# Linear layers whose products are traced one group behind the split of their weights

## The chip, the cores and the metric

The program runs on one core of a Trainium2 chip. The metric is the device time of one execution in microseconds (us), the median of three runs. Engines are named as the profile names them: PE (TensorE, matmuls), PEld (its weight loads), DVE (VectorE), ACT (ScalarE), POOL (GpSimd), SP (SyncE, whose queue issues most DMAs).

## The reference, cut to what matters

256 tokens of width 1024 go through a hybrid layer (an SSD scan and a sparse attention side by side, then a mixture of 32 experts of which each token takes 2) and through two layers of a second block for the tokens and for a context of 256 (grouped attention, then latent attention, each with a gated convolutional feed-forward part of width 2816). What matters here is that nearly all of it is matrix products with float32 weights from DRAM, and that the experts' products are small:

```python
for e in range(N_EXPERTS):
    he = jax.nn.silu(t @ w_g[e]) * (t @ w_u[e])
    out = out + combine[:, e:e + 1] * (he @ w_d[e])
```

The kernel computes an expert only for the tokens that chose it, 32, 64 or 128 positions for each.

## The kernel before, in words

**A linear layer.** Weights come in groups. `weight` (L183) loads a tile of 128 x 512 float32 (256 KB) through SP's queue into a ring of 14 buffers named `raw`. `split_weight` (L188) turns a group into a high part (`whi`, L198, on ACT) and the rest (`wlo`, L199, on DVE); both rings have 4 buffers (L106), and a group of a linear layer takes two of each. `mm3` (L214) then makes three products for each block: `whi` x high activations (L217), `wlo` x high (L218), `whi` x low (L219). `lin_fm` (L221) puts features on partitions: chunks of 256 columns, groups of 4 blocks of 128 rows, so 24 products a group and two groups for an inner size of 1024. `lin_tm` (L247) puts tokens on partitions, in groups of 1024 // width blocks. The products add up in the PSUM ring `lin`.

**Evictions.** A finished chunk isn't evicted at once. Its eviction is put on the list `late`, and `flush` (L204), at the end of the next `split_weight` or at the end of the layer, traces it. So the order of tracing is: split of a group, eviction of the chunk that ended before it, products of the group.

**Side work.** Each linear layer is a generator that yields the PE time it has traced. `weave` (L137) and `mix` (L157) put units of other generators between its steps in fixed shares: the scan, the sparse attention, the columns of the adaptive norms (`ada_quad`, L385), the attentions. In one stretch the roles are turned: `mix(self.experts(), (ctx, 2.1))` (L1930) makes the experts the main work and the context's linear layers (`layer0_ctx`, L1663, with `residual` and `ffn`) the side work. A unit of four experts of 32 positions (`expert_block`, L1306, products at L1317 and L1339) is two rounds of four products, one in each of the four column tiles of PE (128 x 32 weights). Their weights (`wx`, L1302) come through SP's queue too. In this part of the program the ring `lin` has two PSUM banks (L1922), later four (L1935).

**What sets the order.** Tracing gives each instruction its rank. A list scheduler then lays out each engine's stream ahead of time: an instruction that it takes to be ready may pass one of an earlier rank that it takes to be waiting. Each engine executes its stream in that order.

The functions that the change touches, with the line numbers of the profile:

Of the kernel before, what the change touches and what calls it, by code (L numbers as in the profile page):

```python
# [16 lines left out]
P = 128  # L17
# [71 lines left out]
# The experts by their rank in number of tokens: the order of the units (rank of group, half) and their blocks.  # L89
# [3 lines left out]
# The 8 KB buffers: those of the second part lie where what the first part keeps there is done early.  # L93
# [5 lines left out]
class Kernel:  # L99
    def __init__(self, tc, I, cst, cst_at, out, dbg=None):  # L100
        self.tc, self.nc, self.I, self.out = tc, tc.nc, I, out
        self.cst_ap, self.cst_at = cst, cst_at
        self.dbg = dbg or (lambda name, ap: None)
        self.V, self.A, self.T, self.G, self.S = (
            tc.nc.vector, tc.nc.scalar, tc.nc.tensor, tc.nc.gpsimd, tc.nc.sync)
        self.bufs = {"raw": 14, "whi": 4, "wlo": 4, "k2": 8, "k1": 5, "s": 11}  # L106
        self.marks, self.late = [], []
        self.room, self.turn = 0, 0
        self.phase_pool, self.phase_bufs = None, {}
# [60 lines left out]
    def passing(self, name, tag):  # L170
        """A constant that is needed only once."""
# [10 lines left out]
    # ---------------------------------------------------------------- weights  # L182
# [5 lines left out]
    def split_weight(self, view):  # L188
        """(hi, lo) of each block of 128 rows of a view [128, n, cols]."""
# [11 lines left out]
        self.flush()  # L201
        return parts

    def flush(self):  # L204
        """Evictions are traced after the next weights' split, which TensorE waits for."""
# [15 lines left out]
    def lin_fm(self, W, c0, ncols, act, evict, k0=0, nk=None, more=False):  # L221
        """out^T: features on partitions. W [K, N] in DRAM; act (hi, lo) [128, nk, 256]."""
        hi_a, lo_a = act
        nk = nk or W.shape[0] // P
        for cc in range(0, ncols, 256):
            ps = self.ps("lin", [P, 2, TOK])
            for kg in range(0, nk, 4):
# [4 lines left out]
                for k in range(n):  # L232
                    for m in range(2):
                        ms = slice(m * P, m * P + P)
                        self.mm3(ps[:, m, :], (parts[k][0][:, ms], parts[k][1][:, ms]), (hi_a[:, kg + k, :], lo_a[:, kg + k, :]),
                                 kg + k == 0 and m == 0, kg + k == nk - 1)
                if kg + n < nk:
                    yield n * 0.66
            def out(cc=cc, ps=ps):
                for m in range(2):  # L240
                    evict(cc // P + m, ps[:, m, :])
            self.late.append(out)
            if cc + 256 >= ncols and not more:
                self.flush()
            yield n * 0.66

    def lin_tm(self, W, c0, ncols, act, evict, chunk=512):  # L247
        """out: tokens on partitions."""
        hi_a, lo_a = act
        nk = W.shape[0] // P  # L250
        for cc in range(0, ncols, chunk):
            w = min(chunk, ncols - cc)
            pss = [self.ps("lin", [P, w]) for _ in range(2)]
            step = 1024 // w
            for kg in range(0, nk, step):
# [3 lines left out]
                for k in range(n):  # L259
                    for t in range(2):  # L260
                        s = slice(t * P, t * P + P)
                        self.mm3(pss[t], (hi_a[:, kg + k, s], lo_a[:, kg + k, s]), parts[k],
                                 kg + k == 0, kg + k == nk - 1)
                if kg + n < nk:
                    yield n * w * 0.0025
            def out(cc=cc, w=w, pss=pss):
                for t in range(2):
                    evict(t, cc, w, pss[t])
            self.late.append(out)
            if cc + w >= ncols:  # L270
                self.flush()
            yield n * w * 0.0025

    # ---------------------------------------------------------------- set-up
# [73 lines left out]
    def load_fm(self, src, h, tag, eng):  # L348
        """[256, 1024] rows of DRAM -> feature-major h [128, 8, 256]."""
# [16 lines left out]
    # ---------------------------------------------------------------- adaLN  # L366
# [11 lines left out]
    def take_bias(self, stg, dst):  # L378
        """The bias into dst [128, slots, 48], to which the products are added."""
# [5 lines left out]
    def ada_quad(self, W, q, dst, rsel):  # L385
        """Columns 2048q..2048q+2047 of silu(c) @ W onto dst [128, slots, 48]."""
# [17 lines left out]
    def ada_start(self, p):  # L404
        """Shift and scale of the first norm for half of the features, in the order of ada1."""
# [20 lines left out]
    def first_act(self, rb):  # L426
        """The first norm and the first two chunks of the token-major projection, by halves of the features as the
        modulation comes in."""
# [4 lines left out]
        def products(half):  # L433
            for c in range(2):
                for k0 in range(4 * half, 4 * half + 4, 2):
                    parts = self.split_weight(W[k0 * P:k0 * P + 2 * P, 5120 + 468 * c:5588 + 468 * c].rearrange(
                        "(k p) n -> p k n", p=P))
                    for k in range(2):
                        for t in range(2):
                            ts = slice(t * P, t * P + P)  # L440
                            self.mm3(pss[c][t], (act[0][:, k0 + k, ts], act[1][:, k0 + k, ts]), parts[k],
                                     k0 + k == 0, k0 + k == 7)
                        yield 1.2
# [32 lines left out]
    # ---------------------------------------------------------------- norms  # L476
    def square_sums(self, h, nt, st, gain=None):
        """Sums of squares over features (32 times them) into the two columns of st: the column tiles of TensorE add up
        a quarter each."""
# [17 lines left out]
    def rms_bcast(self, h, nt, dim):  # L497
        """1/rms over features, one column per token, on all partitions (PSUM [128, 256])."""
# [11 lines left out]
    def spread(self, r, n):  # L510
        """Columns of r, one value per token, along the free dimension of all partitions."""
# [11 lines left out]
    def modulation(self, gain, ada, slot, vs, vsc):  # L523
        """gain * (1 + scale) and shift, [128, 8] each."""
# [15 lines left out]
    # ---------------------------------------------------------------- first block: projections  # L540
# [26 lines left out]
    def rope(self, x, nh, t, outs):  # L567
        """x [128, nh, 64] token-major, half-split rotation; written to each of outs."""
# [12 lines left out]
    def project_tm(self, act, pss):  # L581
        """dt, q, k/v, gates of the first block, tokens on partitions; the first two chunks are in pss."""
# [8 lines left out]
    def conv_silu(self, dst, ps, wname, bname, m, nm, taps):  # L591
        """Causal depthwise convolution over tokens, then silu."""
# [20 lines left out]
    # ---------------------------------------------------------------- SSD  # L613
# [40 lines left out]
    def ssd(self):  # L654
        """The chunked scan; y (with the skip) replaces the x channels. Yields where TensorE would wait."""
# [90 lines left out]
    def ssd_gate(self, act, sums):  # L746
        """y * silu(z), and its squares summed by group into sums [2][128, 2, 256]."""
# [35 lines left out]
    # ---------------------------------------------------------------- NSA  # L783
# [141 lines left out]
    def nsa_attend(self):  # L925
        """Selected and window branches (causal both: every block is chosen and the window spans the sequence)."""
# [85 lines left out]
    def tanh_gates(self, act, c0, sg):  # L1012
        """tanh(x / 2): the sigmoid is half of one more."""
# [78 lines left out]
    # ---------------------------------------------------------------- mixture of experts  # L1092
    def router(self, h):
# [35 lines left out]
        def top(x):  # L1129
            """softmax over the 8 columns; its sorted values and their places."""  # L1130
# [55 lines left out]
        # experts by their number of tokens: place of each expert and expert of each place  # L1186
# [67 lines left out]
    def one_hots(self, d, cols):  # L1254
        """For positions 256 d + cols: token x position, by first and second choice, [128, 2, n] per half of tokens."""
# [10 lines left out]
    def expert_gather(self, d, tag, n=256):  # L1266
        """The normalised tokens at positions 256 d.., features on partitions."""
# [15 lines left out]
    def expert_weights(self, part, experts):  # L1283
        """One part of the experts' weights, 256 rows of gate or up or 256 columns of down each."""
# [21 lines left out]
    def expert_block(self, xg, d, q, experts, sizes):  # L1306
        """The 128 positions 256 d + 128 q..: one expert's, or several experts' in the column tiles of TensorE."""
# [42 lines left out]
    def expert_spread(self, d, q):  # L1350
        """What takes the block's rows back to the tokens, position x token, and the rows' weights."""
# [29 lines left out]
    def experts(self):  # L1381
        """The two experts with the most tokens have 128 positions each, the next two 64, the others 32."""
# [13 lines left out]
    def experts_rest(self):  # L1396
        """Tokens beyond those positions: blocks of 32 from position 1536."""
# [580 lines left out]
```

## Time and profile before

| | us |
|---|---|
| runs, median of 3 (lowest, highest) | 1768.83 (1765.71, 1769.4) |
| profiled execution, first to last instruction | 1765.9 |
| PE busy | 1690.6 (96%) |
| DVE, ACT busy | 1272.3 (72%), 917.8 (52%) |

The profile has no other time of the profiled execution than its span; the median of the runs lies 2.9 us above it. PE's busy time is the union of its matmuls, which are pipelined: a product of 256 columns is shown with 0.28 us, and the next begins 0.12 us after it began. A matmul of the experts, whose operands are plain float32, stands in the trace as two records; in the order below it is one row.

### The profile page before, as it was taken

To read this page: it belongs to the slowest core of one execution; us is meant where nothing else is said; L and a number is where in the kernel's file an instruction comes from. 1 tells how busy PE (TensorE), PEld (TensorE's weight loads), DVE (VectorE), ACT (ScalarE), POOL (GpSimd) and SP (SyncE) were. 2 spreads that over 40 slices of the span, in tenths; PEclk is the share of its full clock that TensorE was granted. 3 is DMA by queue.
4 is the path that set the end of the run, shared out by engine and by line. 5 is a ranking of instruction groups with operands and counts; after the bars stand their busy time and mean duration, and the time that the engine had idled before them with its cause. 6 is when DMAs were issued, how large, how long until landed. Compare 5 with 4: busy or idle time off the path is not lost. (4 is left out here: it accounts for less than half of the span.)

```text
span 1765.9 us, 36466 instructions
## 1 busy us (share of the span) xinstructions
PE 1690.6 (96%) x12980; PEld 1379.4 (78%) x12980; DVE 1272.3 (72%) x3070; ACT 917.8 (52%) x1901; POOL 42.4 (2%) x48
## 2 busy tenths in 40 slices
PE   7999999999999999999999898999999989999998
PEld 3898777767876578888887554688999866789997
DVE  3997687675667768757756466968777788777876
ACT  2666446863443544534434252656665566556654
POOL 0000000100001000000000001000000000000000
PEclk8999999999999999999999988999999999999999
DMA  9756956849966997998999886234566432246662
GB/s 321 212 150 195 322 175 191 253 133 306 317 201 207 323 318 240 329 328 268 325 347 346 258 299 229 90 122 138 178 183 183 141 120 72 59 141 183 180 186 72
DMA packets 344962, 381.54 MB, mean 216 GB/s; under 512 B 27353, under 2 KB 298454, under 8 KB 344774
## 3 DMA queue, kind: packets, MB, share of 16 engines
q1 hardware_dynamic: 339456, 376.47, 67.2%
q10 hardware_dynamic: 5174, 1.97, 0.4%
q8 instruction: 104, 1.70, 0.4%
q0 software_dynamic: 144, 0.71, 0.1%
q14 instruction: 84, 0.69, 0.1%
HBM read 378.00 MB, written 1.05 MB: 215 GB/s over the span
## 5 line engine op out<-in xcount | busy, mean ns | idle before, releaser
L198 ACT CAST whi<-raw 128x512 fp32r<-128x512 f32 (+2 forms) x752 | 453.9, 610 | 383.9 <-PE lin L219 219.5
L199 DVE TENSOR_TENSOR wlo<-raw,whi 128x512 fp32r<-128x512 f32 (+2 forms) x752 | 502.4, 678 | 161.5 <-ACT whi L198 148.6
L217 PE MATMUL lin<-XA,whi 128*128 128x256 f32 x768 | 220.1, 287 | 1.7 <-ACT XA L465 1.7
L219 PE MATMUL lin<-XA,whi 128*128 128x256 f32 x768 | 219.0, 286 | 0.0
L218 PE MATMUL lin<-XA,wlo 128*128 128x256 f32 x768 | 218.9, 285 | 0.0
L217 PE MATMUL lin<-A,whi 128*128 128x256 f32 x576 | 168.4, 292 | 2.7 <-DVE k L598 1.9
L218 PE MATMUL lin<-A,wlo 128*128 128x256 f32 x576 | 163.5, 284 | 0.0
L217 PEld LDWEIGHTS lin<-XA,whi 128*128 128x128 f32 x768 | 149.3, 194 | 2.6 <-ACT XA L465 2.5
L218 PEld LDWEIGHTS lin<-XA,wlo 128*128 128x128 f32 x768 | 149.2, 194 | 0.7 <-issue 0.4
L219 PEld LDWEIGHTS lin<-XA,whi 128*128 128x128 f32 x768 | 148.9, 194 | 0.3
L217 PEld LDWEIGHTS lin<-A,whi 128*128 128x128 f32 x576 | 109.9, 191 | 33.8 <-issue 14.1
L219 PE MATMUL lin<-A,whi 128*128 128x256 f32 x448 | 127.7, 285 | 0.0
L217 PE MATMUL lin<-CA,whi 128*128 128x256 f32 x416 | 122.0, 293 | 0.3 <-ACT whi L198 0.2
L218 PE MATMUL lin<-CA,wlo 128*128 128x256 f32 x416 | 118.2, 284 | 1.1 <-DVE wlo L199 1.1
L219 PE MATMUL lin<-CA,whi 128*128 128x256 f32 x416 | 117.9, 283 | 0.0
L218 PEld LDWEIGHTS lin<-A,wlo 128*128 128x128 f32 x576 | 110.1, 191 | 0.9 <-issue 0.7
L1621 ACT ACTIVATE cv<-lin,vecs 128x256 f32<-128x256 f32 x132 | 73.9, 560 | 63.0 <-PE lin L219 52.7
L219 PE MATMUL lin<-XB,whi 128*128 128x256 f32 x352 | 99.4, 286 | 0.1
L1622 DVE SCALAR_TENSOR_TENSOR cv<-lin,vecs,cv 128x255 f32<-128x255 f32 x132 | 63.3, 480 | 49.4 <-ACT cv L1621 49.1
L217 PE MATMUL lin<-XB,whi 128*128 128x256 f32 x352 | 98.7, 283 | 0.0
L218 PE MATMUL lin<-XB,wlo 128*128 128x256 f32 x352 | 98.4, 283 | 0.0
L217 PEld LDWEIGHTS lin<-CA,whi 128*128 128x128 f32 x416 | 79.2, 190 | 15.5 <-issue 6.5
(534 smaller groups left out, 3835.0 us busy)
## 6 DMA issues: line engine op xcount, KB each, us to landing
raw<-in_ffn_w_up_dram SPq DMA_DIRECT2D x264, 256.0 KB
raw<-in_ada_w_dram SPq DMA_DIRECT2D x192, 256.0 KB
raw<-in_ffn_w_down_dram SPq DMA_DIRECT2D x132, 256.0 KB
raw<-in_w_in_dram SPq DMA_DIRECT2D x112, 256.0 KB
wx<-in_w_exp_gate_dram SPq DMA_DIRECT2D x112, 256.0 KB
wx<-in_w_exp_up_dram SPq DMA_DIRECT2D x112, 256.0 KB
wx<-in_w_exp_down_dram SPq DMA_DIRECT2D x112, 256.0 KB
raw<-in_w_ada_dram SPq DMA_DIRECT2D x96, 256.0 KB
```

The lines of the kernel that those rows point to most:

```text
L198: self.A.copy(hi, raw)
L199: self.V.tensor_tensor(lo, raw, hi.bitcast(F32), OP.subtract)
L217: mm(out, whi, ahi, start=first, stop=False, skip_group_check=True)
L218: mm(out, wlo, ahi, start=False, stop=False, skip_group_check=True)
L219: mm(out, whi, alo, start=False, stop=last, skip_group_check=True)
L1621: A.activation(acc, ps, AF.Identity, bias=self.v(f"fb{i}", m), scale=self.v(f"fw{i}1", m))
L1622: V.scalar_tensor_tensor(acc[:, 1:], ps[:, 0:TOK - 1], self.v(f"fw{i}0", m), acc[:, 1:], OP.mult, OP.add)
```

## The change

Each group is split first; then what an earlier group has left to evict is traced; then the products of the group before. So products are traced one group later than the split of their weights, and the eviction of a finished chunk is traced after the split of the group after the next. `behind` keeps the last group's products in `self.ahead`; `settle`, at the end of a layer that isn't followed by more of it, traces what is left. The list is one for all generators, so the split of one layer can bring out the products of another. `lin_tm` takes at most two blocks in a group, which differs for 288 columns alone (three blocks before). The diff, cut to its core (it takes out comments and docstrings too):

```diff
@@ split_weight
             parts += [(hi[:, j, :], lo[:, j, :]) for j in range(m)]
+        return parts
+
+    def behind(self, products):
         self.flush()
-        return parts
+        last, self.ahead = self.ahead, products
+        if last:
+            last()
+
+    def settle(self):
+        self.behind(None)
+        self.flush()
@@ lin_fm
+        def products(cc, kg, n, parts, held):
+            if kg == 0:
+                held.append(self.ps("lin", [P, 2, TOK]))
+            ps = held[0]
+            for k in range(n):
+                for m in range(2):
...
+            if kg + n == nk:
+                self.late.append(lambda: [evict(cc // P + m, ps[:, m, :]) for m in range(2)])
         for cc in range(0, ncols, 256):
-            ps = self.ps("lin", [P, 2, TOK])
+            held = []
             for kg in range(0, nk, 4):
                 n = min(4, nk - kg)
                 r0 = (k0 + kg) * P
                 parts = self.split_weight(
                     W[r0:r0 + n * P, c0 + cc:c0 + cc + 256].rearrange("(k p) n -> p k n", p=P))
...
-            if cc + 256 >= ncols and not more:
-                self.flush()
-            yield n * 0.66
+                self.behind(lambda a=(cc, kg, n, parts, held): products(*a))
+                if kg + n == nk and cc + 256 >= ncols and not more:
+                    self.settle()
+                yield n * 0.66
@@ lin_tm (otherwise as lin_fm)
-            step = 1024 // w
+            step = min(2, 1024 // w)
@@ first_act, products(half)
-                    for k in range(2):
...
-                        yield 1.2
+                    self.behind(some)
+                    yield 2.4
+            self.settle()
@@ experts_rest
+        self.settle()
         total = self.nc.values_load(self.over[0:1, 16:17], min_val=0, max_val=16)
```

Every engine executes the same instructions before and after but for ACT, which loads its function table two times less. The order differs. On PE, near the end of the experts' stretch, a unit of gate or up products of four experts (`acc<-wx,xg`) stood in one piece between the context's products (`lin<-CA`) before:

```order
L218 MATMUL lin<-CA_8571,wlo 128x256
L219 MATMUL lin<-CA_8572,whi 128x256
L1317 MATMUL acc<-wx,xg 32x256 x8
L217 MATMUL lin<-CA_8571,whi 128x256
L218 MATMUL lin<-CA_8571,wlo 128x256
L219 MATMUL lin<-CA_8572,whi 128x256
```

In the changed kernel single products of such a unit stand between the context's products (`lin<-CB`, the same layers a little later) there:

```order
L1332 MATMUL acc<-wx,xg 32x256
L227 MATMUL lin<-CB_11924,whi 128x256
L1332 MATMUL acc<-wx,xg 32x256
L228 MATMUL lin<-CB_11924,wlo 128x256
L229 MATMUL lin<-CB_11925,whi 128x256
L227 MATMUL lin<-CB_11924,whi 128x256
L228 MATMUL lin<-CB_11924,wlo 128x256
L229 MATMUL lin<-CB_11925,whi 128x256
L227 MATMUL lin<-CB_11924,whi 128x256
L228 MATMUL lin<-CB_11924,wlo 128x256
L1332 MATMUL acc<-wx,xg 32x256
L229 MATMUL lin<-CB_11925,whi 128x256
```

From the last unit that stands alike in both to the end of the context's work, the same 128 expert products stood in 18 runs before and stand in 44 runs now. Counted in rounds (up to four products that follow each other, one for each column tile), they are 36 before and 61 now. In the whole program the runs of these products (with weights `wx`) go from 100 to 128, the rounds from 288 to 313. The order of the loads in SP's queue is the same in that stretch.

On DVE, where the latent attention's projection of the context (288 columns) begins beside the first feed-forward part, the low parts of the first weights stood like this before, after the last pieces of the norm (`CA`) and between evictions (`hx`):

```order
L466 SCALAR_TENSOR_TENSOR CA_15970<-k_15995,ada_69,CA_15969 128x256
L1089 SCALAR_TENSOR_TENSOR hx<-lin,ada_68,hx 128x256
L466 SCALAR_TENSOR_TENSOR CA_15970<-k_15999,ada_69,CA_15969 128x256
L1089 SCALAR_TENSOR_TENSOR hx<-lin,ada_68,hx 128x256
L199 TENSOR_TENSOR wlo<-raw,whi 128x288 x2
```

They are the second and the third tile of a group of three. Now a group has two, both stand ahead of the evictions:

```order
L481 SCALAR_TENSOR_TENSOR CA_15945<-k_15970,ada_69,CA_15944 128x256
L199 TENSOR_TENSOR wlo<-raw,whi 128x288
L481 SCALAR_TENSOR_TENSOR CA_15945<-k_15974,ada_69,CA_15944 128x256
L199 TENSOR_TENSOR wlo<-raw,whi 128x288
L1104 SCALAR_TENSOR_TENSOR hx<-lin,ada_68,hx 128x256 x2
```

The splits have moved ahead of two evictions of the other layer. On PE nothing but a handful of neighbours changes places in the two feed-forward parts of the tokens (about 1230 to 1406 us and from 1540 us to the end in the profile before).

## Rows read from the trace of the kernel before

**Rows 1.** The page, part 1: busy time, share and instructions of each engine.

```profile
PE 1690.6 (96%) x12980; PEld 1379.4 (78%) x12980; DVE 1272.3 (72%) x3070; ACT 917.8 (52%) x1901; POOL 42.4 (2%) x48
```

**Rows 2.** Stretches of the program: busy us of each engine, clock, DMA share.

```profile
core 0: us, PE busy (x) PEld busy (x) DVE busy (x) ACT busy (x) POOL busy (x), PEclk, DMA share, GB/s
0.00:44.00 44.00, 32.38 (x206) 16.28 (x207) 14.46 (x43) 11.89 (x21) 1.64 (x6) 0.88 0.91 321
...
860.00:933.00 73.00, 73.00 (x714) 62.24 (x713) 47.34 (x102) 29.22 (x54) 0.00 (x0) 1.00 1.08 339
933.00:997.00 64.00, 60.81 (x575) 47.93 (x577) 38.10 (x84) 22.94 (x45) 0.00 (x0) 1.00 1.06 340
997.00:1012.00 15.00, 10.95 (x110) 5.50 (x102) 6.75 (x16) 1.76 (x3) 0.00 (x0) 0.97 0.59 185
...
1230.00:1406.00 176.00, 175.96 (x1441) 174.28 (x1440) 137.62 (x269) 108.45 (x206) 0.00 (x0) 1.00 0.58 174
```

**Rows 3.** Waits of PE in the whole span: us in total, times, longest.

```profile
PE lin L219 <- DVE wlo L199: 4.4, 4, 2.7
...
PE lin L218 <- DVE wlo L199: 1.1, 2, 0.9
...
PE lin L217 <- ACT whi L198: 0.9, 2, 0.7
```

**Rows 4.** Timeline of PE around a whole expert unit: start, us, line.

```profile
886.44 0.28 PE L218 MATMUL lin<-CB,wlo 128*128 128x256 f32 x1
886.56 0.28 PE L219 MATMUL lin<-CB,whi 128*128 128x256 f32 x1
886.77 1.07 PE L1317 MATMUL acc<-wx,xg 128*32 128x256 f32 x16
887.77 0.39 PE L217 MATMUL lin<-CB,whi 128*128 128x256 f32 x1
888.00 0.28 PE L218 MATMUL lin<-CB,wlo 128*128 128x256 f32 x1
```

**Rows 5.** Timeline of PE around one round of an expert unit.

```profile
974.31 0.28 PE L219 MATMUL lin<-CB,whi 128*128 128x256 f32 x1
974.52 0.64 PE L1317 MATMUL acc<-wx,xg 128*32 128x256 f32 x8
975.09 0.38 PE L217 MATMUL lin<-CB,whi 128*128 128x256 f32 x1
975.31 0.28 PE L218 MATMUL lin<-CB,wlo 128*128 128x256 f32 x1
975.52 0.63 PE L1317 MATMUL acc<-wx,xg 128*32 128x256 f32 x6
976.08 0.39 PE L217 MATMUL lin<-CB,whi 128*128 128x256 f32 x1
976.30 0.28 PE L219 MATMUL lin<-CB,whi 128*128 128x256 f32 x1
```

**Rows 6.** Timeline of PE at 1170 us: in brackets idle time before it, and releaser.

```profile
1170.45 0.53 PE L219 MATMUL lin<-wlo,CA 128*128 128x288 f32 x2 [2.71 <-DVE wlo L199]
```

**Rows 7.** DVE's groups from 1230 to 1406 us: busy us, mean ns of one.

```profile
L199 DVE TENSOR_TENSOR wlo<-raw,whi 128x512 fp32r<-128x512 f32 (+1 forms) x120 | 81.7, 685 | 23.4 <-ACT whi L198 21.3
L1622 DVE SCALAR_TENSOR_TENSOR cv<-lin,vecs,cv 128x255 f32<-128x255 f32 x38 | 18.2, 479 | 11.4 <-ACT cv L1621 11.4
```

**Rows 8.** PE's waits from 933 to 997 us; ahead of them L218's, in rows 3.

```profile
...
PE aux L1326 <- DVE k L1323: 1.0, 1, 1.0
PE aux L1372 <- ACT o_e L1344: 0.6, 1, 0.6
PE acc L1339 <- DVE hT L1328: 0.3, 1, 0.3
PE lin L217 <- ACT whi L198: 0.2, 1, 0.2
```

More of the change, by code (lines that the diff above doesn't have):

```diff
@@ L106, in __init__ @@
         self.bufs = {"raw": 14, "whi": 4, "wlo": 4, "k2": 8, "k1": 5, "s": 11}
-        self.marks, self.late = [], []
+        self.marks, self.late, self.ahead = [], [], None
         self.room, self.turn = 0, 0
@@ L224, in lin_fm @@
         nk = nk or W.shape[0] // P
+        def products(cc, kg, n, parts, held):
[4 more added lines that the diff above has]
+                for m in range(2):
+                    ms = slice(m * P, m * P + P)
+                    self.mm3(ps[:, m, :], (parts[k][0][:, ms], parts[k][1][:, ms]), (hi_a[:, kg + k, :], lo_a[:, kg + k, :]),
+                             kg + k == 0 and m == 0, kg + k == nk - 1)
+            if kg + n == nk:
+                self.late.append(lambda: [evict(cc // P + m, ps[:, m, :]) for m in range(2)])
         for cc in range(0, ncols, 256):
-            ps = self.ps("lin", [P, 2, TOK])
+            held = []
             for kg in range(0, nk, 4):
@@ L231, in lin_fm @@
                     W[r0:r0 + n * P, c0 + cc:c0 + cc + 256].rearrange("(k p) n -> p k n", p=P))
[L232 to L237, printed above, removed]
-                    yield n * 0.66
[L239 to L242, printed above, removed]
-            if cc + 256 >= ncols and not more:
-                self.flush()
-            yield n * 0.66
+                self.behind(lambda a=(cc, kg, n, parts, held): products(*a))
+                if kg + n == nk and cc + 256 >= ncols and not more:
+                    self.settle()
+                yield n * 0.66
     def lin_tm(self, W, c0, ncols, act, evict, chunk=512):
@@ L250, in lin_tm, with products @@
         nk = W.shape[0] // P
+        def products(cc, w, kg, n, parts, pss):
+            if kg == 0:
+                pss += [self.ps("lin", [P, w]) for _ in range(2)]
+            for k in range(n):
+                for t in range(2):
+                    s = slice(t * P, t * P + P)
+                    self.mm3(pss[t], (hi_a[:, kg + k, s], lo_a[:, kg + k, s]), parts[k], kg + k == 0, kg + k == nk - 1)
+            if kg + n == nk:
+                self.late.append(lambda: [evict(t, cc, w, pss[t]) for t in range(2)])
         for cc in range(0, ncols, chunk):
             w = min(chunk, ncols - cc)
-            pss = [self.ps("lin", [P, w]) for _ in range(2)]
-            step = 1024 // w
+            pss = []
+            step = min(2, 1024 // w)
             for kg in range(0, nk, step):
@@ L258, in lin_tm @@
                     W[kg * P:(kg + n) * P, c0 + cc:c0 + cc + w].rearrange("(k p) n -> p k n", p=P))
[L259 to L272, printed above, removed]
+                self.behind(lambda a=(cc, w, kg, n, parts, pss): products(*a))
+                if kg + n == nk and cc + w >= ncols:
+                    self.settle()
+                yield n * w * 0.0025
     def setup(self):
@@ L437, in products, with some @@
                         "(k p) n -> p k n", p=P))
-                    for k in range(2):
[L439 to L442, printed above, removed]
-                        yield 1.2
+                    def some(c=c, k0=k0, parts=parts):
+                        for k in range(2):
+                            for t in range(2):
+                                ts = slice(t * P, t * P + P)
+                                self.mm3(pss[c][t], (act[0][:, k0 + k, ts], act[1][:, k0 + k, ts]), parts[k],
+                                         k0 + k == 0, k0 + k == 7)
+                    self.behind(some)
+                    yield 2.4
+            self.settle()
         def norm(half):
@@ L1396, in experts_rest @@
     def experts_rest(self):
+        self.settle()
         total = self.nc.values_load(self.over[0:1, 16:17], min_val=0, max_val=16)
```

## The prediction

> **What bounds the kernel now.** I read the busy times first: PE is busy for 96% of the span, 75 us short of it [rows 1]. The table by stretch says where those 75 us lie [rows 2]: 11.6 in the first 44 us, where the weights are still coming in (44 less 32.38), about 4 between 997 and 1012 us, where the experts' work ends, and next to nothing in the stretch from 860 to 933 us (73.00 of 73) and in the first feed-forward part from 1230 to 1406 us (175.96 of 176). The reader is to see that PE's stream decides nearly everywhere. So a step of this change counts only if it takes time out of PE's stream or puts some into it.
>
> The waits come next, since the change aims at one kind of them: a product that waits for the high or the low part of its weights. There are three rows of it, 4.4 + 1.1 + 0.9 = 6.4 us in eight waits, and the longest is 2.7 us [rows 3]. That is all that earlier splits can give back directly, 0.36% of the span.
>
> Last I read the timeline of PE at the end of the experts' stretch, because the order shows there what the change puts in. Products of 256 columns begin 0.12 us apart (886.44, 886.56). A whole unit of four experts, eight products in two rounds of the four column tiles (16 records), stands between the product that begins at 886.56 and the second product behind it at 888.00: 1.44 us, less the two steps of 0.12 that the products would take anyway, is **1.20 us for a whole unit** [rows 4]. One round alone takes from 974.31 to 975.31: 1.00 less 0.24 is **0.76 us for a run of one round**, and the next one on the same rows, from 975.31 to 976.30, 0.75 [rows 5]. The difference, 0.44 us, is a round; what is left, 0.76 less 0.44, is 0.32 us for going from products of 128 columns of weights to the column tiles and back. It is paid once in each run.
>
> **The change part by part.** *Splits one group earlier.* This is meant to end the 6.4 us of waits. How much of them goes I can't read from the trace of before, so I bound it: all 6.4 at best, nothing at worst. I take half, 3.2. The longest wait, 2.71 us, ends at 1170.45 us [rows 6], where the context's latent projection begins beside the feed-forward part; the low parts of its weights stood behind the last pieces of the norm and behind evictions on DVE. They move ahead of two evictions, but the first of them now stands behind most of the norm's pieces too, where it stood ahead of them before, so part of that wait stays. The waiting instruction is a product, and behind it in PE's stream are the feed-forward products, which have their operands: the wait is paid in full.
>
> *Evictions one group later.* No instruction is added. An eviction now has one more split ahead of it on ACT and DVE. On DVE that is two low parts of 0.685 us, 1.37 us [rows 7]. In the feed-forward stretch of the tokens DVE is busy 137.62 of 176 us [rows 2], the ring of PSUM has four banks there, and PE's order is nearly the same: I cost it at nothing. What hides it is the chunk in between, 48 products of 0.12, or 5.8 us. If this cover is gone the PSUM ring stalls PE (third rival).
>
> *Side work in another order on PE.* This is the largest term, and it is a cost. The list scheduler has cut units of the experts into pieces: 100 runs of their products become 128, and 288 rounds (up to four products in a row) become 313. 26 of the 28 added runs and all 25 added rounds lie in one stretch, the last of the context's work beside the experts (933 to 997 us before). A single expert product uses one of four column tiles, and the others are idle while it runs, so a round that is cut is paid twice. The sum: 28 x 0.32 + 25 x 0.44 = 9.0 + 11.0 = **20.0 us**. The bounds: if a cut round cost nothing beyond the switch, 28 x 0.32 = 9.0; if each added run cost what a whole unit does, 28 x 1.20 = 33.6. I take 20.0, as the two rows of single rounds (0.76 and 0.75) agree [rows 5] and lie in the very stretch. Is this beside other work or on the path? PE has no spare time there: 60.81 of 64 us busy, and the waits from 933 to 997 us are all named, 3.2 us, not one of them for a load (the two waits of L218 lie here) [rows 2, 3, 8]. The stretch must end before the experts' last sums, the branch and the norm of the next layer begin, so what it grows by is added to the span. The most that could be given back is PE's idle time from 997 to 1012 us, 15 less 10.95, 4 us, if weights that had longer to arrive cut it.
>
> *The loads.* SP's stream keeps its order in that stretch. The loads fill the DMA engines there (share 1.06, 340 GB/s) [rows 2]; a slower PE asks less of them. Nothing is added for it.
>
> *The rest.* Two blocks in a group in place of three for 288 columns: eight blocks in four groups for three, in the same two low parts a step; nothing. The first layer's products start while PE waits for weights anyway (32.38 busy of 44). The scan and the sparse attention from 44 to 530 us, and the latent attention, have their units shifted by some instructions in both directions. I put these at 0, give or take 3 us.
>
> *The sum.* 1765.9 - 3.2 + 20.0 = 1782.7 us for the span; with the 2.9 us by which the median of the runs lies above the span, 1785.6 or **1786 us**, 1.0% slower. Its own range takes the bounds: at the short end all waits gone, only the switches paid and 3 us won elsewhere, 1765.9 - 6.4 + 9.0 - 3 + 2.9 = 1768; at the long end 1765.9 + 33.6 + 3 + 2.9 = 1805. The ends need everything to fall on one side; I hold 1775 to 1797 for the likely part.
>
> **The rivals.** *Slack that the busy share hides: no change.* From 933 to 997 us PE loads weights for 47.93 of 64 us, 75%; in the feed-forward stretch for 174.28 of 176, 99% [rows 2]. If the missing quarter, 16 us, were time in which PE has nothing to do, the cut units would fall into it, and only the waits would count: 1765.9 - 3.2 + 2.9 = 1765.6. The Trainium skill, Trainium Kernel Development and Optimization, section Performance Expectations, says that matmul busy time is a bad measure of how near a kernel is to its limit, because matmuls are pipelined, and that the busy share of the weight loads is a good one; by that rule this rival is the likelier case. Against it stand the starts: products follow each other every 0.12 us right up to a unit and from the second product behind it [rows 4], so the quarter is the units themselves, whose loads are short, and the switches. Chance 0.13.
>
> *Weights that come late: faster.* The DMA engines are full from 860 to 997 us. If the weights of single experts came late there, whole units would make PE wait for the last of four, and cut ones would let the context's products run meanwhile. Then the cut units would cost nothing, all split waits would go, and the time would be 1768.8 - 6.4 = 1762.4. It decides if an added run costs less than 6.4 / 28 = 0.23 us net. For it: the full DMA. Against it: no wait of PE in the stretch is for a load [rows 8], and the order of the loads is the same. Chance 0.10.
>
> *Evictions that come too late: much slower.* Beside the experts the ring of products has two banks. The first group of a chunk needs the bank of the chunk before the last, whose eviction now stands behind one more split. 37 chunks of the context (74 groups in the order) run there. If half of the added 1.37 us showed at each, 37 x 0.685 = 25 us would come on top: 1811. It decides where the eviction's chain, two high and low parts and then some six steps of ACT and DVE of about half a microsecond [rows 7], exceeds the 5.8 us of a chunk. Against it: an expert unit stands between most groups and lengthens that time. Chance 0.05.
>
> **How the numbers follow.** The forecast has the remaining 0.72. Slower by over 0.2%, which is 3.5 us and about what a measurement of this kernel can tell from no change, is the forecast and the last rival: 0.77. Within it is the slack: 0.13. Faster is the late weights: 0.10. The range must reach down to the slack (1765.6) only in part: from 1766, leaving the faster case out, to 1800, leaving out the late evictions and the tail of the bounds.
>
> **What would show it.** If I am right, the stretch that was 64 us long (933 to 997) is 80 to 85, PE busy throughout, with runs of two records of `acc<-wx,xg` between single products, each costing about 0.7; the feed-forward stretch stays at 176 us; the three rows of split waits sum to 2 to 5 us. I am wrong if that stretch keeps its length, if two records between products cost under 0.4 us, if PE's waits name loads of `wx` there, or if products there wait for evictions of `lin`.

## The result and the profile after

The changed kernel takes 1789.1 us (median of four runs, 1782.4 to 1789.6) against 1768.3 for the kernel before (1765.7 to 1769.4, with one run more than ahead of the prediction): a ratio of 1.0114, 95% interval 1.0096 to 1.0132. The forecast was 1786. The profiled execution is the quickest of the four: 1782.42 us, with a span of 1780.6; the spans of the other three are 1787.0 to 1787.7. So what the two profiles differ by, 14.7 us, is less than the medians' 20.8, and a part of it has to be looked for in the spread of the runs (last section).

Part 1 of the changed kernel's page, which answers to [rows 1]:

```profile
PE 1706.8 (96%) x12980; PEld 1381.6 (78%) x12980; DVE 1275.5 (72%) x3070; ACT 916.8 (51%) x1899; POOL 44.1 (2%) x48
```

PE has the same 12,980 records and is busy 16.2 us longer; the busy times of its weight loads, DVE and ACT differ by at most 3.2 us. Where the 16.2 us lie is seen by stretch (changed kernel; columns as in [rows 2]). The first fence is of one answer, the second of another, from the last product of a pair of experts, `acc<-raw,hT`, to the end of the experts' products:

```profile
0.00:44.00 44.00, 30.16 (x202) 13.84 (x202) 13.41 (x41) 11.62 (x20) 1.64 (x6) 1.00 0.89 302
860.00:933.00 73.00, 73.00 (x715) 61.77 (x713) 45.68 (x93) 29.42 (x54) 0.00 (x0) 1.00 1.09 348
933.00:1012.00 79.00, 76.37 (x545) 51.43 (x543) 40.09 (x87) 24.61 (x49) 0.00 (x0) 1.00 0.86 270
1012.00:1030.00 18.00, 15.19 (x149) 8.71 (x149) 5.96 (x14) 1.76 (x3) 0.00 (x0) 1.00 0.55 176
...
1245.00:1421.00 176.00, 176.00 (x1442) 174.55 (x1441) 137.84 (x269) 108.90 (x206) 0.00 (x0) 1.00 0.60 174
```

```profile
857.50:1028.10 170.60, 165.58 (x1416) 123.03 (x1412) 92.80 (x197) 56.98 (x108) 0.00 (x0) 1.00 0.94 298
```

The same stretch of the kernel before:

```profile
858.50:1008.90 150.40, 144.78 (x1392) 115.80 (x1388) 91.29 (x197) 55.05 (x104) 0.00 (x0) 1.00 1.04 331
```

The feed-forward part has not changed (176 us in both), and ahead of 860 us little has: the first expert product comes 2.4 us later (574.6 for 572.2 us), and from there to this last stretch it is 282.9 us in place of 286.3. The stretch itself is 20.2 us longer, and PE is busy 20.8 us longer in it. It holds 24 products more (1416 against 1392 records): those of the last group, which come one group later. At 0.12 us each they are 2.9 us that are moved and not added, so 17.3 us are a cost. The DMA share falls (1.04 to 0.94), and the clock is full in both: it isn't the loads. Behind the stretch the changed kernel's profile is 4.5 us shorter (752.5 against 757.0 us), so that 14.7 us are left of the difference.

What PE does there (the changed kernel's timeline of PE: start, us, line; a unit of experts that is cut in four, from its second piece to its last):

```profile
988.26 0.28 PE L229 MATMUL lin<-CB,whi 128*128 128x256 f32 x1
988.47 0.62 PE L1332 MATMUL acc<-wx,xg 128*32 128x256 f32 x2
989.02 0.39 PE L229 MATMUL lin<-CB,whi 128*128 128x256 f32 x1
989.24 0.28 PE L227 MATMUL lin<-CB,whi 128*128 128x256 f32 x1
...
989.72 0.28 PE L228 MATMUL lin<-CB,wlo 128*128 128x256 f32 x1
989.93 0.62 PE L1332 MATMUL acc<-wx,xg 128*32 128x256 f32 x2
990.48 0.39 PE L229 MATMUL lin<-CB,whi 128*128 128x256 f32 x1
990.70 0.28 PE L227 MATMUL lin<-CB,whi 128*128 128x256 f32 x1
...
991.29 0.28 PE L229 MATMUL lin<-CB,whi 128*128 128x256 f32 x1
991.50 1.05 PE L1332 MATMUL acc<-wx,xg 128*32 128x256 f32 x10
992.49 0.38 PE L227 MATMUL lin<-CB,whi 128*128 128x256 f32 x1
992.71 0.28 PE L228 MATMUL lin<-CB,wlo 128*128 128x256 f32 x1
```

A single product of an expert (2 records) stands between the products that begin at 988.26 and 989.24 us: 0.98, and less the two steps of 0.12 that is 0.74 us, as much as a full round of four did in [rows 5] (0.76). A remainder of five (10 records) takes from 991.29 to 992.71, which is 1.18 us, nearly as much as a whole unit (1.20, [rows 4]). Cut into 1, 1, 1 and 5 a unit costs 3 x 0.74 + 1.18 = 3.4 us in place of 1.2. Between the pieces shown PE doesn't wait: the context's products follow at 0.12 us.

The waits, first those of the whole span that answer to [rows 3], then those from 933 to 1030 us, which answer to [rows 8] (us in total, times, longest):

```profile
PE lin L227 <- DVE k L613: 3.4, 3, 1.5
...
PE lin L229 <- DVE wlo L199: 2.0, 3, 1.4
...
PE lin L227 <- ACT whi L198: 1.7, 2, 1.1
...
PE lin L228 <- DVE wlo L199: 0.8, 2, 0.6
```

```profile
PE aux L1341 <- DVE k L1338: 1.2, 2, 1.0
PE aux L1387 <- ACT o_e L1359: 1.2, 2, 0.8
PE lin L227 <- ACT whi L198: 1.1, 1, 1.1
PE lin L228 <- DVE wlo L199: 0.6, 1, 0.6
PE acc L1354 <- DVE hT L1343: 0.9, 2, 0.6
```

The split waits are 4.5 us (6.4 before). The wait for `k` in the first row is another: L613 is the causal convolution of the scan's input, through which a finished chunk is evicted (`k<-lin`), so here a product waits until an eviction has freed its bank. Before, this row was

```profile
PE lin L217 <- DVE k L598: 1.9, 2, 1.3
```

In the last stretch of the experts no wait is for a load, and none for an eviction of `lin`.

### The profile page after: what moved, and what is told of

The parts are those of the page before. It is cut to its first block, busy times and chain, and to the rows that moved or that the text cites. A ratio compares the mean times of both kernels' runs of the same rounds, so it can differ in the third digit from the quotient of the medians.

```text
span 1780.6 us, 36602 instructions
## 1 busy us (share of the span) xinstructions
PE 1706.8 (96%) x12980; PEld 1381.6 (78%) x12980; DVE 1275.5 (72%) x3070; ACT 916.8 (51%) x1899; POOL 44.1 (2%) x48
## 5 line engine op out<-in xcount | busy, mean ns | idle before, releaser
L198 ACT CAST whi<-raw 128x512 fp32r<-128x512 f32 (+3 forms) x752 | 455.0, 610 | 472.6 <-PE lin L229 329.0
L199 DVE TENSOR_TENSOR wlo<-raw,whi 128x512 fp32r<-128x512 f32 (+3 forms) x752 | 503.5, 677 | 201.6 <-ACT whi L198 195.5
L227 PEld LDWEIGHTS lin<-XA,whi 128*128 128x128 f32 x768 | 149.4, 195 | 2.6 <-ACT XA L480 2.4
L227 PEld LDWEIGHTS lin<-A,whi 128*128 128x128 f32 x576 | 110.0, 191 | 31.6 <-ACT whi L198 11.7
L229 PEld LDWEIGHTS lin<-A,whi 128*128 128x128 f32 x448 | 85.6, 191 | 0.9 <-issue 0.7
```

Of the source, the lines that this page charges most:

```text
L198: self.A.copy(hi, raw)
L199: self.V.tensor_tensor(lo, raw, hi.bitcast(F32), OP.subtract)
L227: mm(out, whi, ahi, start=first, stop=False, skip_group_check=True)
L229: mm(out, whi, alo, start=False, stop=last, skip_group_check=True)
```

## The experiments

The runs of one group share a chip with runs of the kernel before, whose medians there were 1767.9 us (for the first four versions below), 1768.2 (the next four) and 1768.9 (the last three). Three questions: is the place of the loss the experts' stretch; is it the cut units, or what cuts them; and which half of the change cuts them.

**The place.** `c_oldexp` is the changed kernel with the old order of tracing beside the experts alone; `d_newexp` has the new order there alone. Both are built from the changed kernel, so `d_newexp` differs from the kernel before in the groups for 288 columns too, which have two blocks.

```diff
@@ behind
+        if self.old and products:
+            self.ahead = None
+            products()
@@ run: c_oldexp (in d_newexp True and False change places, and it starts True)
+                    self.old = True
                     self.mix(self.experts(), (ctx, 2.1))
+                    self.old = False
```

Expected of `c_oldexp`: 

> The changed kernel, with the old tracing of products and evictions only for the context's layers beside the experts (102 runs and 286 rounds in the program). Theory: all of the loss goes, and what the change gives elsewhere is left: the split waits that it shortens are worth up to 4 us, so 1762 to 1769 us. Rival (the loss lies in the late products and evictions of the other layers, or in the banks that they hold): 1780 us or more.

Expected of `d_newexp`: 

> The kernel before, with the new tracing only for the context's layers beside the experts (132 runs and 320 rounds in the program, 32 more of each than before). Theory: 32 x .32 + 32 x .44 = 24.3 us by the prediction's prices, some 4 us of it given back after the experts: 1783 to 1793 us. Rival (the loss lies elsewhere): 1765 to 1771 us.

Measured: `c_oldexp` 1768.55 us, ratio to the kernel before 0.9997 (0.9985 to 1.0010); `d_newexp` 1789.75 us, 1.0123 (1.0101 to 1.0145). The whole loss is beside the experts, and the change everywhere else is worth nothing that can be measured: the split waits of `c_oldexp` are 3.8 us, 2.6 less than before, and its time doesn't show them. Both versions switch the order from the first expert product on; their windows from the last product of a pair to the end of the experts are 149.4 us (`c_oldexp`) and 169.5 (`d_newexp`), so the loss lies in that last stretch.

**Whole units.** PE's order can be held, so that a unit's products stay together. `a_whole` and `b_whole` hold every unit beside the experts in the changed kernel and in the kernel before.

```diff
+    def whole(self, last="unit"):
+        ins = getattr(self, last)
+        return self.tc.issue_after(ins) if ins is not None and self.beside else nullcontext()
@@ mm3: behind the last product of the unit traced before
+        with self.whole():
...
@@ expert_block, products of gate and up, and of down: behind the last product of a linear layer
+                with self.whole("product"):
...
+                self.unit = ins.ins
```

Expected of `a_whole`: 

> The changed kernel, but with TensorE held to the traced order between a unit of eight expert products and the products of the context's linear layers, so that no unit is cut. Theory (cut units cost the time): in the program the runs of four-tile expert products go from 128 back to 97 and the rounds from 313 to 282, so 31 x .32 + 31 x .44 = 23.6 us less than the changed kernel by the prediction's prices: 1763 to 1772 us, and the stretch from the last product on raw columns to the end of the experts shrinks from 184.6 us to 160 to 168. Rival (units are cut because their weights come in late, and TensorE only fills the wait): a unit that is held together then waits for its loads, TensorE's idle time in that stretch grows by about what the cuts cost, and the time stays at 1782 to 1792 us.

Expected of `b_whole`: 

> The kernel before, with the same hold on the order between units and products beside the experts. It takes its runs from 100 to 97 and its rounds from 288 to 283. Theory: 3 x .32 + 5 x .44 = 3.2 us less than before, 1763 to 1768 us. Rival (the held order makes TensorE wait for late weights): 1770 us or more, with new waits for loads in the stretch of the experts.

Measured: `a_whole` 1773.75 us, 1.0037 (1.0022 to 1.0052), so 15.4 less than the changed kernel; `b_whole` 1782.4 us, 1.0079 (1.0060 to 1.0098), 14.5 more than the kernel before. The first came out a little above its range, the second missed by far. The last stretch of the experts is 150.1 us in `a_whole` (170.6 with cut units), as the theory has it (about 164 us by the measure of the expectation, from the last `acc<-raw,xg`); in `b_whole` it is 151.0 (150.4 before), where five runs fewer were to make it shorter. What was lost in `b_whole` lies earlier: from 573 to 874 us PE is idle for 15.5 us (301.10 less 285.61), and in the same part of the kernel before for 5.4. The waits of PE in `b_whole` from the first expert product to the last of a pair (573 to 874 us) begin with

```profile
PE aux L1334 <- DVE k L1331: 5.4, 4, 2.4
PE acc L1348 <- DVE hT L1336: 3.7, 7, 1.5
```

which are the transposition that waits for silu times up, and the down products that wait for `hT`. Before, these two were 1.3 and 2.3 us there. No wait is for a load of weights: the rival's mechanism (late weights) isn't it. These waits are idle time of PE, so while a held down unit waits, the products behind it wait too. So a hold on the order isn't free; that part of what the scheduler cuts fills such waits is an inference from this.

**Only gate and up units of four experts held.** `a_gateup` and `b_gateup` take the hold from the down units and from the experts with 64 or 128 positions.

```diff
@@ expert_block, products of gate and up (those of down are left as they were)
-                with self.whole("product"):
+                with self.whole("product", len(ws) == 4):
```

Expected of `a_gateup`: 

> The changed kernel with the same hold, on gate and up units of four experts alone. Theory: after the last product on raw columns 20 runs of gate and up products stand in place of 45, and 23 rounds fewer; down units stay cut. 25 runs at .66 us are 16.5 us less than the changed kernel: 1770 to 1776 us. Rival (weights come late and TensorE only fills the wait): 1780 us or more.

Expected of `b_gateup`: 

> The kernel before, with the order held beside the experts only for the gate and up units of four experts: down units, and units of one or two experts, are left to the scheduler. The earlier kernel that held every unit had the same stretch after the last product on raw columns (151.0 us against 150.4 of before) and lost its 14 us earlier, between the first expert product and that one (301.1 against 286.3 us), where TensorE waited for the silu products and for hT. Theory: those waits go with the hold on the down units and on the large experts, so the time is at most that of before, and the 5 runs that are fewer after the last product on raw columns (20 against 25, at .66 us as the changed kernel and its held version show) give 3.3 us: 1761 to 1768 us. Rival (any hold makes TensorE wait, for late weights): 1772 us or more.

Measured: `a_gateup` 1767.46 us, 0.9994 (0.9980 to 1.0008), the time of before; its stretch is 153.1 us, 17.5 less than with cut units where 16.5 were expected. By the medians it is 21.7 below the changed kernel, and so below its range too. The 4.2 us between the two aren't shown by the profiles, in which what lies outside the stretch is 3.3 us longer than in the changed kernel; they are in the spread of the runs. `b_gateup` 1770.35 us, 1.0015 (1.0004 to 1.0027): the 3.3 us expected didn't come, and it is above its range. Its stretch is 150.4 us, as before. PE is busy 143.25 us there, 1.5 less than before, and idle 1.5 more: these few cuts seem to have stood where PE would wait.

**The price of a cut by itself.** `cut_1_7` and `cut_4_4` start from `b_gateup` and cut each gate and up unit once, with one product of the linear layer between the pieces.

```diff
+CUT = 1            # 4 in cut_4_4
@@ mm3
-            mm(out, whi, ahi, ...)
+            one = mm(out, whi, ahi, ...)
+        self.finish_unit(one.ins)        # products[CUT:] of the unit, held behind this product
@@ expert_block
+                    with self.whole("product"):
+                        self.unit = some(products[:CUT])
+                    self.rest = lambda: some(products[CUT:])
```

Expected of `cut_1_7`: 

> The kernel before with the held gate and up units, each of which is cut once on purpose: its first product, then one product of the context's linear layer, then the other seven. Nothing else is moved. Against the same kernel with whole units it has 30 runs and 30 rounds more. Theory (a cut has a price of its own): by the prediction's prices 30 x .32 + 30 x .44 = 22.8 us over that kernel, by the run lengths of the two profiles (.55 us for one product, .99 for seven, 1.00 for eight, and some .15 on the linear product behind it) 30 x .69 = 20.7 us. Rival (a cut only fills a wait and costs nothing): within 3 us of that kernel.

Expected of `cut_4_4`: 

> The same, cut in the middle: four products, which are one round of the column tiles, then one product of the linear layer, then the other four. It has 32 runs more than the kernel with whole units, and one round fewer. Theory: the switch alone is paid, by the prediction 32 x .32 = 10.2 us over the kernel with whole units, by the run lengths (.57 us for four, 1.00 for eight, and .15) 32 x .29 = 9.3 us; so some half of what cutting after one product costs. Rival one (the price is all switch, the round is free): the same as the cut after one product. Rival two (the price is all round): nothing, within 2 us of whole units.

Measured: `cut_1_7` 1790.65 us, 1.0128 (1.0104 to 1.0151), 20.3 over `b_gateup` (20.7 expected); `cut_4_4` 1782.9 us (1776.6 to 1784.0), 1.0087 (1.0065 to 1.0110), 12.6 over it (9.3 expected). A free cut, a price that is all switch and a price that is all round are refuted. The experts' stretch (last product of a pair to the end) of `b_gateup`, `cut_1_7` and `cut_4_4`:

```profile
861.60:1012.00 150.40, 143.25 (x1393) 115.49 (x1389) 91.34 (x197) 55.09 (x104) 0.00 (x0) 1.00 1.05 332
```

```profile
875.10:1034.80 159.70, 153.10 (x1393) 118.09 (x1389) 91.38 (x197) 54.97 (x104) 0.00 (x0) 1.00 0.98 312
```

```profile
866.40:1020.10 153.70, 146.90 (x1393) 114.54 (x1389) 91.40 (x197) 55.06 (x104) 0.00 (x0) 1.00 1.02 324
```

All have the same 1393 records. The timelines have 30 runs of four-expert products in this stretch in the first and 46 in either of the others. 16 cuts after one product cost 9.3 us, 0.58 each; 16 in the middle cost 3.3, 0.21 each. So of a cut about 0.21 us is the switch and 0.37 the round that is opened twice. The other half of the cuts lies earlier. With them, from the first expert product to the end of the experts, it is (the same three in the same order)

```profile
573.60:1012.00 438.40, 425.41 (x3864) 339.98 (x3863) 293.36 (x682) 182.14 (x377) 3.97 (x3) 1.00 0.98 310
```

```profile
575.90:1034.80 458.90, 446.91 (x3864) 346.11 (x3863) 294.64 (x682) 182.07 (x377) 3.97 (x3) 1.00 0.94 296
```

```profile
574.40:1020.10 445.70, 433.93 (x3864) 338.66 (x3863) 294.30 (x682) 181.94 (x377) 3.97 (x3) 1.00 0.96 305
```

30 cuts after one product cost 20.5 us here, 0.68 each, and 32 in the middle 7.3, 0.23 each: 0.23 for the switch and 0.45 for the round. Each of these rests on one profile. By the medians of the whole runs a cut costs 0.68 and 0.39; the second rests on runs that spread by 7 us, of which the profiled one is the quickest.

**The halves of the change.** `late_evict` traces evictions after the next group's products and leaves the products where they were; `late_prod` traces the products one group later and the evictions right behind them. In both an eviction is still traced ahead of the next split. So the step that the prediction priced, one more split ahead of an eviction on ACT and DVE, is in neither of them; it is what the changed kernel has more than `late_prod`. Counted in the traces, of 716 instructions of DVE and ACT that read `lin` to evict it, 297 stand behind more split parts in the changed kernel than before, 46 in `late_prod` and none in `late_evict`.

```diff
@@ behind: late_evict
+        late, self.late = self.late, []
+        if products:
+            products()
+        for e in late:
+            e()
@@ behind: late_prod (the flush moved behind the products)
         last, self.ahead = self.ahead, products
         if last:
             last()
+        self.flush()
```

Expected of `late_evict`: 

> Half of the change: the evictions of a linear layer's sums are traced after the next group's products, and those products stay at once behind the split of their weights. 100 runs and 288 rounds of expert products, as before. Theory (the loss is in the cut units, and only late products cut them): as before, 1764 to 1771 us. Rival (the sums hold their banks longer, so that TensorE waits for a free bank): 1775 us or more, with waits of lin products for evictions.

Expected of `late_prod`: 

> The other half: the products of a group are traced after the next group's split, and the eviction of their sum right behind them. 129 runs and 314 rounds of expert products, as in the changed kernel (128 and 313). Theory: the whole loss, 1782 to 1792 us. Rival (late evictions have their part in it): 1770 to 1780 us.

Measured: `late_evict` 1765.76 us, 0.9988 (0.9978 to 0.9998); `late_prod` 1787.56 us, 1.0098 (1.0078 to 1.0117). The late products are the whole loss. The expectation of `late_evict` calls it half of the change, but it moves evictions behind products only and says nothing of the added split. For that there are two other comparisons. The changed kernel (1789.1 us) is within the spread of `late_prod`, and the last stretch of the experts is 170.6 us in the one and 170.0 in the other. And the wait for the convolution's eviction is 3.3 or 3.4 us, three times, in the changed kernel and in each version that keeps its order outside the experts' part (`c_oldexp`, `a_whole`, `a_gateup`, `a_fourtile`), and 1.9 or 2.0 us, twice, in all others, `late_prod` and `late_evict` among them. (In `late_evict` one product more waits for an eviction, a residual's, for 2.4 us after the experts.) So an eviction behind one more split costs about 1.5 us at this place and nothing that shows beside the experts. `late_evict` is the only version whose interval lies below the kernel before, by 0.12%, less than what a measurement of this kernel can tell from no change.

**The last cuts.** `a_fourtile` holds the down units of four experts as well (the line of `a_gateup` at both places).

Expected: 

> The changed kernel with the order held for gate, up and down units of four experts, and the large experts left to the scheduler. Against the version that held the gate and up units alone (1767.5 us) it has 10 runs of down products fewer after the last product on raw columns. Theory one (a cut costs .66 us wherever it is): 6.6 us less, 1758 to 1764 us, which would be the fastest of all. Theory two (a held down unit passes its wait for hT on to the linear products behind it, as where every unit was held: 7.8 us of waits for k and hT): what the cuts give is lost to those waits, 1765 to 1772 us.

Measured: 1768.62 us, 0.9996 (0.9982 to 1.0009). Theory two fits. Its stretch is the shortest for these 1417 records:

```profile
864.40:1014.30 149.90, 143.54 (x1417) 117.87 (x1413) 93.33 (x198) 57.26 (x107) 0.00 (x0) 1.00 1.07 339
```

but before it, from 572 to 864 us, PE waits again for `k` and `hT`:

```profile
PE aux L1349 <- DVE k L1346: 2.6, 2, 1.6
...
PE acc L1363 <- DVE hT L1351: 2.1, 5, 0.5
```

where `a_gateup` has 0.9 us for `hT` and none for this `k`. What the whole down units give in the stretch, 3.2 us (153.1 to 149.9), is lost ahead of it.

## Why the prediction was right, step by step

*PE's stream decides nearly everywhere.* It held: the loss (20.8 us by the medians) stands in the profile as PE time in one stretch, in which PE is busy 97% (165.58 of 170.60).

*Splits one group earlier, half of 6.4 us gained.* The waits went from 6.4 to 4.5 us, within the 2 to 5 that the prediction named, so 1.9 us went in place of 3.2. The longest is 1.4 us in place of 2.7. But the gain didn't reach the end: `c_oldexp`, in which the change is in force everywhere but beside the experts, is at 0.9997. The waits for evictions (next step) took back nearly as much. The profiles give a hint of where it went: in the six versions whose products are late outside the experts' part, the time behind the last expert product is 753.8 us in the mean and 756.4 in the seven others, but the first expert product comes at 575.3 us and in the others at 573.2. With one profile each and overlapping ranges that isn't shown. This step was too hopeful, by some 3 us.

*Evictions one group later, nothing.* It held where the prediction looked, in the feed-forward stretch and beside the experts; there no product waits for an eviction of `lin`, and with that the third rival (1811 us) falls. It didn't look at the scan's input (about 90 to 178 us), whose chunks are evicted through a convolution and whose ring `lin` has two banks too: there the waits for evictions grew from 1.9 to 3.4 us, and a residual's eviction added one of 0.3. So this term is some 1.8 us and not nothing.

*Cut units, 20.0 us.* The mechanism is shown: with the old tracing in that stretch alone the loss is gone, with the new one in that stretch alone it is all there, with the units held together it is gone too, and cuts made on purpose cost as much. The size: in the stretch the timelines have 61 runs and 103 rounds of four-expert products in place of 35 and 78, the 26 and 25 of the prediction, and they cost 17.3 us, 0.67 each. The prediction's prices for these, 26 x 0.32 + 25 x 0.44 = 19.3, are 2 us more. The cuts on purpose give, in this stretch alone, 26 x 0.21 + 25 x 0.37 = 14.7 us, and by all of them 26 x 0.23 + 25 x 0.45 = 17.2, which is the measured cost. So the price of the round was right (0.44), and what was too high is the switch, 0.32 in place of about 0.2; why a round cost less in the last stretch than earlier isn't shown.

*The stretch.* It was to grow from 64 us to 80 to 85, by 16 to 21. From the product that stood at 933.5 us to the end of the experts it grew from 75.4 to 95.6 us, by 20.2, of which 2.9 are the products that moved into it. Up to 4 us were to come back from PE's idle time after it at most; by the timelines nothing did before the experts' end. The runs of two records between single products are there, at 0.74 us ("about 0.7").

*The rest, 0 give or take 3 us.* It held: 0.9997 in `c_oldexp`.

*The sum* came out at 1786 against 1789.1. Two errors of about 3 us stand in it, one for each side: the gain on the split waits that didn't arrive, in part because of the evictions put at nothing, and a cost of the cuts that was 2.7 us high (20.0 for 17.3). That they cancel is luck. What is left, some 3 us, is in the size of the spread of the runs and stays open.

*The rivals.* Slack (1765.6) is refuted by `d_newexp` and `cut_1_7`: the cut units didn't fall into a free quarter of the span. The Trainium skill, Trainium Kernel Development and Optimization, section Performance Expectations, names the busy share of the weight loads as a good measure of how near a kernel is to its limit. This trace differs: in the experts' stretch of the changed kernel PEld's share is 123.03 of 170.60, 72%, lower than the 77% of before (115.80 of 150.40), and yet what the cuts added there is paid in full. The cuts on purpose lower the share too, from 77% in `b_gateup` (115.49 of 150.40) to 74% in `cut_1_7` (118.09 of 159.70): where column tiles alternate with full-width products, a lower share didn't mean room. Late weights (1762.4) is refuted as a cause, as no wait there is for a load; but a weaker form of it fits the runs: where units wait, for `hT` or for silu times up, a cut that fills the wait costs nothing. `b_gateup` took cuts away from the kernel before, `a_fourtile` from `a_gateup`, and both gained nothing.

## What to carry to other kernels

Count how often small work in column tiles is interrupted: here a round of four tiles took 0.55 us with one product in it and 0.57 with four, so a scheduler that slips full-width products between them adds a cost that no wait and no instruction count shows. When a change of tracing order is to bring products later or earlier, look at the order of the engine it is not aimed at, in the stretch with the most kinds of work. To hold an order by hand, hold only what has its operands: a held unit that waits makes all that is behind it wait.

## What the runs showed of the hardware

A cut has two prices that could be told apart: 0.21 to 0.23 us for going from full-width products to column tiles and back, and 0.37 to 0.45 us for a round opened again. A round takes PE as long with one product as with four: 0.55 us (988.47 to 989.02) and 0.57 (974.52 to 975.09, [rows 5]).

The spread between executions comes at least partly from the granted clock. `late_prod` (1787.56 us) has nearly the changed kernel's order on PE, and nearly the same stretch at the end of the experts (170.0 us); its profiled span is 7.8 us longer, 1788.4, and 7.4 of that it has by the start of that stretch (864.9 against 857.5 us). The same 60 us of the changed kernel and of `late_prod`:

```profile
560.00:620.00 60.00, 53.82 (x434) 32.79 (x436) 41.12 (x115) 26.02 (x74) 6.55 (x4) 0.97 0.88 282
```

```profile
560.00:620.00 60.00, 53.49 (x359) 30.77 (x359) 34.30 (x98) 22.54 (x62) 6.55 (x4) 0.83 0.74 235
```

With a mean granted clock of 0.83 in place of 0.97 PE gets through 75 records less in the same time; in the rest of that part, to 857 us, both have 1.00. By finer windows of `late_prod` the clock is at 0.50, the level of 1.2 GHz, here:

```profile
586.00:595.00 9.00, 9.00 (x32) 4.12 (x32) 4.14 (x11) 3.30 (x14) 0.00 (x0) 0.50 1.11 352
...
606.00:612.00 6.00, 6.00 (x28) 1.99 (x25) 3.11 (x13) 1.81 (x9) 0.00 (x0) 0.50 0.41 143
```

Just ahead of both stretches PE sat idle, for 2.03 us up to 584.98 and for 1.79 us up to 605.42; in both it was then busy throughout, and the clock rose to 1.00 behind them. The changed kernel waits at the same two places, for 1.45 and 1.79 us, and behind its waits the clock is 1.00 (585 to 595 and 601 to 612 us). So the same wait may be followed by the lower clock or not. Profiles of two kernels are best compared stretch by stretch, and in stretches at the full clock.
